# Two matmuls with a GELU between: eight of the opening's twelve loads move to GpSimd's queue and cast on the way

## The chip, the cores and the metric

The kernel runs on one core of a Trainium2 chip. The metric is the device time of one execution in microseconds (us), as the median of several runs. The profile is of one further execution on the same kind of chip.

## The reference

The inputs are `a` (1024 x 1024), `b` (1024 x 2048) and `c` (2048 x 1024), all float32. The kernel must compute

```python
h = np.matmul(a, b)
h = 0.5 * h * (1 + np.tanh(np.sqrt(2 / np.pi) * (h + 0.044715 * h ** 3)))
return np.matmul(h, c).astype(np.float32)
```

that is, a matmul, the tanh form of GELU, and a second matmul.

## The kernel before

**Stages.** All operands of matmuls are brought to bfloat16 (or to float32r for sums of blocks). The first matmul is made transposed: h's columns lie on the partitions, in 16 tiles of 128, in two halves of 512 rows of `a` each (`hT[0]`, `hT[1]`). The first four of the 16 tiles are made in the *opening*, by plain matmuls (`mm1`, `block`). The other twelve follow in two stages (`zero` for four tiles, `one` for eight), and the second matmul is a third stage (`two`). These three stages use a scheme of seven block products in place of eight (`Seven`, `seven`): sums and differences of blocks are made on VectorE and the products on TensorE (line 197).

**The opening.** `a` must be transposed, so that k lies on the partitions. It is loaded in eight pieces a(h, q): rows of half h, columns 256 q to 256 q + 255, which is two tiles of k. The left 512 columns of `b` are loaded in four pieces b(q) of two k tiles each. Before the change the twelve loads (512 KB each) all stand on SyncE's queue, in the order a(0,0), b(0), a(1,0), and then a(0,q), b(q), a(1,q) for q = 1, 2, 3 (lines 69 to 82). They land as float32 in `sta` and `stb`. From there

- `cast_a(h, q, engines)` casts a piece of `a` to bfloat16 into a small buffer `ab` (two of them), as a whole or in two halves on VectorE or ScalarE (lines 99 and 101);
- `turn(h, q, bank, ab)` transposes it on TensorE, four 128 x 128 blocks at a time, into a PSUM bank `pt` (line 132), and VectorE copies each of its two halves to `aT` (line 133). It is a generator: each `next` does one half, so that products can be put between the halves;
- `cast_b(k)` casts one k tile of `b` on ScalarE into `b1` (line 139);
- `block(h, tiles, ks)` issues the products of these k tiles for output tiles in banks `ps[h, t]` (line 105).

The order of all this is written out by hand (lines 214 to 294): for each q, products for half 0 with the k tiles 2q and 2q + 1, the two halves of turn(1, q), products for half 1, the two halves of turn(0, q + 1). Each engine runs its own instructions in the order in which they are written. `stir` issues products on a constant tile before the first data arrive. The banks: ps[0, 0..3] are banks 0 to 3, ps[1, 0..2] are banks 4 to 6; turn(0, 0) uses bank 4 before that, and nearly all others use bank 7 for both of their halves.

`zero.t1(4, part)` (line 155, on VectorE) makes the first difference of blocks from `aT`, a quarter at a time, between the turns of the opening.

**GpSimd's queue.** It holds a tiny copy into `gate` (line 84), which waits until a(1, 2) has landed, and behind it fourteen loads that cast from float32 to bfloat16 inside the transfer: two for the right half of `b1`, four for `b2` (lines 89 to 93), eight for `c_sb` (line 95). These need no cast on an engine.

Of the kernel before, what the change touches and what calls it, by code (L numbers as in the profile page):

```python
# [9 lines left out]
F32 = mybir.dt.float32  # L10
F32R = mybir.dt.float32r
BF16 = mybir.dt.bfloat16
# [7 lines left out]
def kernel(ctx, tc, a, b, c, out):  # L20
    nc = tc.nc
    M, K = a.shape
    _, N = b.shape
    _, P = c.shape
    H = 512
# [3 lines left out]
    av = a.rearrange("(mt p) k -> p mt k", p=128)  # L29
    bv = b.rearrange("(kt p) n -> p kt n", p=128)  # L30
# [9 lines left out]
    def slot(tag, shape, dt, name):  # L40
        return big.tile(shape, dt, name=name, tag=tag)

    def bank(i, shape=(128, H), dt=F32, name="ps"):
        return pp.tile(list(shape), dt, name=name, tag=f"bank{i}", padded_shape=None)

    def pieces(tag, bufs, shape, dt, name):
        return small.tile(shape, dt, name=name, tag=tag, bufs=bufs)
# [5 lines left out]
    gate = consts.tile([128, 1], F32, name="gate")  # L53
# [7 lines left out]
    b1 = slot("b1", [128, KT, 1024], BF16, "b1")  # L61
# [2 lines left out]

    KH = KT // 2
    stb = slot("x0", [128, KT, H], F32, "stb")
    sta = [slot(f"x{i}", [128, 2, 2, 4, 256], F32, "sta") for i in (1, 3)]

    def load_a(h, q):
        nc.sync.dma_start(out=sta[q // 2][:, h, q % 2],  # L70
                          in_=av[:, 4 * h:4 * h + 4, ds(q * 256, 256)])

    def load_b(q):
        nc.sync.dma_start(out=stb[:, 2 * q:2 * q + 2], in_=bv[:, 2 * q:2 * q + 2, 0:H])

    load_a(0, 0)
    load_b(0)
    load_a(1, 0)
    for q in range(1, 4):
        load_a(0, q)  # L80
        load_b(q)
        load_a(1, q)

    nc.gpsimd.tensor_copy(gate, sta[1][:, 1, 0, 3, 0:1])
    nc.scalar.activation(g, warm[:, 0:1], AF.Gelu_apprx_tanh)


    for k in range(0, KT, 4):
        nc.gpsimd.dma_start(out=b1[:, k:k + 4, H:], in_=bv[:, k:k + 4, ds(H, H)])
    for n in range(2):  # L90
        for k in range(0, KT, 4):
            nc.gpsimd.dma_start(out=b2[:, k:k + 4, ts(n, H)],
                                in_=bv[:, k:k + 4, ds(1024 + n * H, H)])
# [3 lines left out]
    def copy(eng, dst, src):  # L97
        if eng is nc.scalar:
            nc.scalar.activation(dst, src, AF.Copy)  # L99
        else:  # L100
            nc.vector.tensor_copy(dst, src)  # L101

    def mm1(p, t, h, ks):
        for k in ks:
            nc.tensor.matmul(p, b1[:, k, ts(t, 128)], aT[:, h, k],  # L105
                             start=(k == 0), stop=(k == KT - 1))
# [12 lines left out]
    def cast_a(h, q, *engs):  # L119

        ab = pieces("ab", 2, [128, 4, 256], BF16, "ab")
        for i, eng in enumerate(engs):
            w = 256 // len(engs)
            copy(eng, ab[:, :, ts(i, w)], sta[q // 2][:, h, q % 2][:, :, ts(i, w)])
        return ab

    def turn(h, q, i, ab):

        pt = bank(i, (128, 2, H), BF16, "pt")
        for n in range(2):  # L130
            for m in range(4):
                nc.tensor.transpose(pt[:, n, ts(m, 128)], ab[:, m, ts(n, 128)], ident)  # L132
            nc.vector.tensor_copy(aT[:, h, 2 * q + n], pt[:, n])  # L133
            yield

    def cast_b(k, n=1):
        for i in range(n):
            r = ds(i * (H // n), H // n)
            nc.scalar.activation(b1[:, k, r], stb[:, k, r], AF.Copy)  # L139

    def block(h, tiles, ks):
        for k in ks:
            for t in tiles:
                mm1(ps[h, t], t, h, (k,))
# [62 lines left out]
    def quarters(b, c0, w):  # L207
        return [[b[:, 0:4, ds(c0, w)], b[:, 4:8, ds(c0, w)]],
                [b[:, 0:4, ds(c0 + w, w)], b[:, 4:8, ds(c0 + w, w)]]]

    zero = Seven(4, quarters(b1, H, 256), BB, [None] * 4, [None] * 4, 2)
    one = Seven(4, quarters(b2, 0, H), BB, [None] * 4, zero.t)

    stir(256, 256, 256, 256)
    tn = turn(0, 0, 4, cast_a(0, 0, nc.vector))
    next(tn)
    stir(256)
    next(tn)
    stir(128)
    cast_b(0, 2)  # L220
    cast_b(1)
    ab = cast_a(1, 0, nc.vector, nc.scalar)
    block(0, range(4), (0,))
    block(0, range(2), (1,))
    tn = turn(1, 0, 7, ab)
    next(tn)
    block(0, range(2, 4), (1,))
    next(tn)
    for t in range(3):
        ps[1, t] = bank(4 + t)  # L230
    zero.t[0], zero.t[1] = pair(2)
    zero.t1(4, 0)
    ab = cast_a(0, 1, nc.scalar, nc.scalar)
    block(1, range(3), (0,))
    tn = turn(0, 1, 7, ab)
    next(tn)
    block(1, range(3), (1,))
    next(tn)
    cast_b(2)
    cast_b(3)  # L240
    ab = cast_a(1, 1, nc.vector, nc.scalar)
    block(0, range(4), (2,))
    block(0, range(1), (3,))
    tn = turn(1, 1, 7, ab)
    next(tn)
    block(0, range(1, 4), (3,))
    next(tn)
    zero.t1(4, 1)
    ab = cast_a(0, 2, nc.scalar, nc.scalar)
    block(1, range(3), (2,))  # L250
    tn = turn(0, 2, 7, ab)
    next(tn)
    block(1, range(3), (3,))
    next(tn)
    cast_b(4)
    cast_b(5)
    ab = cast_a(1, 2, nc.vector, nc.scalar)
    block(0, range(4), (4,))
    block(0, range(1), (5,))
    tn = turn(1, 2, 7, ab)  # L260
    next(tn)
    block(0, range(1, 4), (5,))
    next(tn)
    zero.t1(4, 2)
    ab = cast_a(0, 3, nc.scalar, nc.scalar)
    block(1, range(3), (4,))
    tn = turn(0, 3, 7, ab)
    next(tn)
    block(1, range(3), (5,))
    next(tn)  # L270
    zero.t1(4, 3)
    cast_b(6)
    cast_b(7)
    ab = cast_a(1, 3, nc.scalar, nc.vector)
    block(0, range(4), (6, 7))
    zero.t2(2, 0)
    for t in range(4):
        gelu(t, 0, ps[0, t])
    ps[1, 3] = bank(7)
    mm1(ps[1, 3], 3, 1, range(2))  # L280
    tn = turn(1, 3, 0, ab)
    next(tn)
    mm1(ps[1, 3], 3, 1, range(2, 5))
    next(tn)
# [210 lines left out]
```

## Time and profile before

| | us |
|---|---|
| Median of 8 runs | 118.21 (117.94 to 118.5) |
| The profiled execution | 118.3 |
| its span, first to last instruction | 116.5 |
| TensorE busy, share of the span | 111.1 (95%) |
| VectorE | 90.4 (78%) |
| ScalarE | 59.3 (51%) |
| GpSimd | 11.0 (9%) |

The granted clock of TensorE was at full speed in every slice of the span. DMA queues moved 17.91 MB; HBM was read for 20.97 MB, more than was written to the core's memory, since a casting load writes half of what it reads.

How to read the views: PE is TensorE (PEld its weight loads), DVE VectorE, ACT ScalarE, POOL GpSimd and SP SyncE; an engine's name with q is its instruction queue. A row of the timeline gives start and length in us, engine and line, operation, the tiles written and read, how often, and in brackets how long the engine stood idle before and what ended that. A row of the stage table gives for a stretch of time the busy time (and instructions) of TensorE, its weight loads, VectorE, ScalarE and GpSimd, then TensorE's clock, the busy share of the DMA engines and the GB/s that they wrote. The chain of work is followed back from the last instruction, at each step to what released it.

### The profile page before, as it was taken

What the parts mean: (1) busy time and instruction counts of PE and PEld (TensorE: products, weight loads), DVE (VectorE), ACT (ScalarE), POOL (GpSimd) and SP (SyncE); (2) the same over time, 40 slices, a digit from 0 to 9 for tenths busy, and PEclk for the clock granted to TensorE, in tenths of its full rate; (3) what the DMA queues carried; (4) which work ended last, traced back from release to release, by engine and by line L of the source; (5) the groups of instructions that cost most, each with busy time, mean ns of one, the idle gap of its engine ahead of it and who ended that gap; (6) DMA issues with size and microseconds to landing.
All of it is one profiled execution on the core that took longest, in us unless ns stands there. A gap on an engine that the chain in (4) does not pass through costs nothing.

```text
span 116.5 us, 1472 instructions
## 1 busy us (share of the span) xinstructions
PE 111.1 (95%) x534; PEld 76.6 (66%) x540; DVE 90.4 (78%) x107; ACT 59.3 (51%) x99; POOL 11.0 (9%) x21
## 2 busy tenths in 40 slices
PE   5989999999999999999999999999999999999980
PEld 4635455545777447888886444588888888888860
DVE  0336566899998999844789999999999986954670
ACT  5066678989369899066699329600033982000000
POOL 2000039723322000000000000000000000000000
PEclk9999999999999999999999999999999999999999
DMA  3999999999999999998000000070000002014993
GB/s 106 270 364 393 396 394 315 205 205 207 206 210 211 210 214 213 209 210 157 2 0 0 0 6 0 0 268 2 0 0 0 0 0 96 0 62 175 367 366 110
DMA packets 13542, 17.91 MB, mean 154 GB/s; under 512 B 736, under 2 KB 8928, under 8 KB 13536
## 3 DMA queue, kind: packets, MB, share of 16 engines
q0 software_dynamic: 5344, 7.34, 35.5%
q1 hardware_dynamic: 8192, 10.49, 25.1%
q8 instruction: 4, 0.07, 0.2%
q14 instruction: 2, 0.02, 0.0%
HBM read 20.97 MB, written 4.19 MB: 216 GB/s over the span
## 4 chain that ended last, share of the span: by engine, by line
PE 90%; DMA 5%; DVE 1%; issue 1%; SPq 0%; ACT 0%
PE ps L197 75%; PE ps L105 12%; DMA stb<-in_b_dram 5%; PE pt L132 3%; SPq L70 0%; DVE aT L133 0%; DVE ot L382 0%; ACT b L139 0%
## 5 line engine op out<-in xcount | busy, mean ns | idle before, releaser
L197 PE MATMUL ps<-x,s 128*128 128x512 f32 x128 | 29.6, 391 | 0.0
L197 PEld LDWEIGHTS ps<-x,s 128*128 128x128 f32 x128 | 24.0, 188 | 5.1
L197 PE MATMUL ps<-x,x 128*128 128x512 f32 x96 | 22.9, 394 | 0.0
L197 PEld LDWEIGHTS ps<-x,x 128*128 128x128 f32 x96 | 18.0, 188 | 3.9
L105 PE MATMUL ps<-aT,b 128*128 128x512 bf16 x62 | 15.8, 379 | 0.7 <-ACT b L139 0.5
L305 ACT ACTIVATE v<-ps 128x512 f32<-128x512 f32 x10 | 6.0, 598 | 19.4 <-PE ps L197 19.4
L197 PE MATMUL ps<-c_sb,hT 128*128 128x512 bf16 (+1 forms) x70 | 14.1, 355 | 0.1
L197 PE MATMUL ps<-x 128*128 128x512 f32 x56 | 13.2, 392 | 0.0
L197 PEld LDWEIGHTS ps<-x 128*128 128x128 f32 x56 | 10.2, 188 | 2.7 <-ACT u L305 0.4
L197 PEld LDWEIGHTS <-hT 128*128 128x128 bf16 x72 | 6.9, 98 | 7.0 <-issue 0.5
L133 DVE COPY aT<-pt 128x512 bf16<-128x512 bf16 x16 | 6.8, 423 | 6.0 <-PE pt L132 6.0
L109 ACT ACTIVATE hT<-ot 128x512 bf16<-128x512 f32 x18 | 10.5, 625 | 1.5 <-DVE ot L310 1.3
L310 DVE TENSOR_TENSOR ot<-ps,u 128x512 f32<-128x512 f32 x10 | 6.8, 690 | 5.2 <-ACT u L305 5.1
L310 DVE TENSOR_TENSOR ot<-ps,v 128x512 f32<-128x512 f32 x10 | 6.7, 688 | 5.2 <-DMA out_dram<-ot 3.8
L197 PE MATMUL ps<-aT,b 128*128 128x512 bf16 x46 | 10.6, 379 | 0.1
L155 DVE TENSOR_TENSOR x<-c_sb 128x1024 fp32r<-128x1024 bf16 x8 | 9.3, 1221 | 0.0
L105 PEld LDWEIGHTS <-b 128*128 128x128 bf16 x64 | 5.5, 98 | 4.8 <-ACT b L139 1.1
L197 PEld LDWEIGHTS <-b 128*128 128x128 bf16 x48 | 4.6, 98 | 5.7 <-issue 0.3
L132 PEld LDWEIGHTS <-ab 128*128 128x128 bf16 x64 | 4.6, 99 | 5.5 <-DVE ab L101 1.9
L99 ACT ACTIVATE ab<-sta 128x512 bf16<-128x512 f32 x10 | 6.0, 625 | 3.4 <-DMA sta<-in_a_dram 3.3
L305 ACT ACTIVATE u<-ps 128x512 f32<-128x512 f32 x10 | 5.9, 596 | 3.4 <-PE ps L197 3.2
L109 ACT ACTIVATE hT<-ps 128x512 bf16<-128x512 f32 x14 | 7.3, 596 | 0.4 <-PE ps L105 0.3
(39 smaller groups left out, 114.9 us busy)
## 6 DMA issues: line engine op xcount, KB each, us to landing
sta<-in_a_dram SPq DMA_DIRECT2D x8, 512.0 KB, 8.5
c_sb<-in_c_dram POOLq DMA_DIRECT2D x8, 512.0 KB, 19.8
b<-in_b_dram POOLq DMA_DIRECT2D x6, 512.0 KB, 11.3
out_dram<-ot SPq DMA_DIRECT2D x12, 256.0 KB, 2.1
stb<-in_b_dram SPq DMA_DIRECT2D x4, 512.0 KB, 8.2
out_dram<-ot SPq DMA_DIRECT2D x8, 128.0 KB, 2.0
```

The lines of the kernel that those rows point to most:

```text
L99: nc.scalar.activation(dst, src, AF.Copy)
L105: nc.tensor.matmul(p, b1[:, k, ts(t, 128)], aT[:, h, k], start=(k == 0), stop=(k == KT - 1))
L109: nc.scalar.activation(hT[h][:, t], p, AF.Gelu_apprx_tanh)
L132: nc.tensor.transpose(pt[:, n, ts(m, 128)], ab[:, m, ts(n, 128)], ident)
L133: nc.vector.tensor_copy(aT[:, h, 2 * q + n], pt[:, n])
L155: nc.vector.tensor_tensor(out=dst[:, r], in0=x[:, r], in1=y[:, r], op=op)
L197: nc.tensor.matmul(p[:, ds(c0, w)], l[:, k, ts(j, 128)], r[:, k, ds(c0, w)], start=(start and k == 0), stop=(k == self.kt - 1), skip_group ...
L305: nc.scalar.activation(st, p, AF.Copy)
L310: nc.vector.tensor_tensor(out=ot, in0=p, in1=st, op=ADD)
```

## The change

Only the first four loads, a(0,0), b(0), a(1,0) and a(0,1), stay on SyncE's queue and are cast on engines as before. The other eight go onto GpSimd's queue, ahead of the fourteen that were there, and cast inside the transfer: b pieces straight into `b1`, a pieces into a new bfloat16 tile `abq` (in the place of the second half of `sta`), from which `turn` reads directly. Their casts on ScalarE and VectorE are gone. The gate copy waits for b(0) in place of a(1, 2). `turn` can take two banks: turn(1, 0) puts its halves into banks 7 and 6 and both are issued one after the other, with the two products that stood between them behind both; the casts of a(0,1) and zero.t1 of the first quarter stand at slightly other places in the order. The rest of the opening keeps its order, written as a loop over q = 1, 2.

```diff
-    sta = [slot(f"x{i}", [128, 2, 2, 4, 256], F32, "sta") for i in (1, 3)]
...
-    load_a(0, 0)
-    load_b(0)
-    load_a(1, 0)
-    for q in range(1, 4):
-        load_a(0, q)
-        load_b(q)
-        load_a(1, q)
-
-    nc.gpsimd.tensor_copy(gate, sta[1][:, 1, 0, 3, 0:1])
+    sta = slot("x1", [128, 2, 2, 4, 256], F32, "sta")
+    abq = slot("x3", [128, 4, 2, 4, 256], BF16, "abq")
...
+    nc.sync.dma_start(out=sta[:, 0, 0], in_=a_part(0, 0))
+    nc.sync.dma_start(out=stb[:, 0:2], in_=b_part(0))
+    nc.sync.dma_start(out=sta[:, 1, 0], in_=a_part(1, 0))
+    nc.sync.dma_start(out=sta[:, 0, 1], in_=a_part(0, 1))
+
+    nc.gpsimd.tensor_copy(gate, stb[:, 1, 0:1])
     nc.scalar.activation(g, warm[:, 0:1], AF.Gelu_apprx_tanh)
 
 
+    def cast_load_a(h, q):
+        nc.gpsimd.dma_start(out=abq[:, q, h], in_=a_part(h, q))
+
+    def cast_load_b(q):
+        nc.gpsimd.dma_start(out=b1[:, 2 * q:2 * q + 2, 0:H], in_=b_part(q))
+
+    cast_load_b(1)
+    cast_load_a(1, 1)
+    for q in range(2, 4):
+        cast_load_a(0, q)
+        cast_load_b(q)
+        cast_load_a(1, q)
     for k in range(0, KT, 4):
         nc.gpsimd.dma_start(out=b1[:, k:k + 4, H:], in_=bv[:, k:k + 4, ds(H, H)])
...
     def turn(h, q, i, ab):
 
-        pt = bank(i, (128, 2, H), BF16, "pt")
+        banks = i if isinstance(i, tuple) else (i,)
+        pts = [bank(x, (128, 2, H), BF16, "pt") for x in banks]
         for n in range(2):
+            pt = pts[n % len(pts)]
...
     block(0, range(4), (0,))
     block(0, range(2), (1,))
-    tn = turn(1, 0, 7, ab)
-    next(tn)
+    for _ in turn(1, 0, (7, 6), ab):
+        pass
+    ab = cast_a(0, 1, nc.scalar, nc.scalar)
     block(0, range(2, 4), (1,))
-    next(tn)
     for t in range(3):
         ps[1, t] = bank(4 + t)
     zero.t[0], zero.t[1] = pair(2)
     zero.t1(4, 0)
-    ab = cast_a(0, 1, nc.scalar, nc.scalar)
     block(1, range(3), (0,))
     tn = turn(0, 1, 7, ab)
     next(tn)
     block(1, range(3), (1,))
     next(tn)
-    cast_b(2)
-    cast_b(3)
-    ab = cast_a(1, 1, nc.vector, nc.scalar)
...
+    for q in range(1, 3):
+        k = 2 * q
+        block(0, range(4), (k,))
+        block(0, range(1), (k + 1,))
+        tn = turn(1, q, 7, abq[:, q, 1])
+        next(tn)
+        block(0, range(1, 4), (k + 1,))
+        next(tn)
+        zero.t1(4, q)
+        block(1, range(3), (k,))
+        tn = turn(0, q + 1, 7, abq[:, q + 1, 0])
+        next(tn)
+        block(1, range(3), (k + 1,))
+        next(tn)
     zero.t1(4, 3)
-    cast_b(6)
-    cast_b(7)
-    ab = cast_a(1, 3, nc.scalar, nc.vector)
     block(0, range(4), (6, 7))
...
-    tn = turn(1, 3, 0, ab)
+    tn = turn(1, 3, 0, abq[:, 3, 1])
```

More of the change, by code (lines that the diff above doesn't have):

```diff
@@ L66, with a_part, b_part @@
     stb = slot("x0", [128, KT, H], F32, "stb")
-    sta = [slot(f"x{i}", [128, 2, 2, 4, 256], F32, "sta") for i in (1, 3)]
[L69 to L74, printed above, removed]
-    load_a(0, 0)
-    load_b(0)
-    load_a(1, 0)
-    for q in range(1, 4):
-        load_a(0, q)
-        load_b(q)
-        load_a(1, q)
-    nc.gpsimd.tensor_copy(gate, sta[1][:, 1, 0, 3, 0:1])
-    nc.scalar.activation(g, warm[:, 0:1], AF.Gelu_apprx_tanh)
+    sta = slot("x1", [128, 2, 2, 4, 256], F32, "sta")
+    abq = slot("x3", [128, 4, 2, 4, 256], BF16, "abq")
+    def a_part(h, q):
+        return av[:, 4 * h:4 * h + 4, ds(q * 256, 256)]
+    def b_part(q):
+        return bv[:, 2 * q:2 * q + 2, 0:H]
+    nc.sync.dma_start(out=sta[:, 0, 0], in_=a_part(0, 0))
[3 more added lines that the diff above has]
+    nc.gpsimd.tensor_copy(gate, stb[:, 1, 0:1])
+    nc.scalar.activation(g, warm[:, 0:1], AF.Gelu_apprx_tanh)
+    def cast_load_a(h, q):
[8 more added lines that the diff above has]
+        cast_load_a(1, q)
     for k in range(0, KT, 4):
@@ L123, in cast_a @@
             w = 256 // len(engs)
-            copy(eng, ab[:, :, ts(i, w)], sta[q // 2][:, h, q % 2][:, :, ts(i, w)])
+            copy(eng, ab[:, :, ts(i, w)], sta[:, h, q][:, :, ts(i, w)])
         return ab
     def turn(h, q, i, ab):
-        pt = bank(i, (128, 2, H), BF16, "pt")
+        banks = i if isinstance(i, tuple) else (i,)
+        pts = [bank(x, (128, 2, H), BF16, "pt") for x in banks]
         for n in range(2):
+            pt = pts[n % len(pts)]
             for m in range(4):
@@ L238 @@
     next(tn)
-    cast_b(2)
-    cast_b(3)
-    ab = cast_a(1, 1, nc.vector, nc.scalar)
[L242 to L270, printed above, removed]
+    for q in range(1, 3):
[12 more added lines that the diff above has]
+        next(tn)
     zero.t1(4, 3)
-    cast_b(6)
-    cast_b(7)
-    ab = cast_a(1, 3, nc.scalar, nc.vector)
     block(0, range(4), (6, 7))
```

## The prediction

> **What bounds the kernel now.** I read the page first: how busy each engine is, and the chain of work that ended last.
>
> ```profile
> PE 111.1 (95%) x534; PEld 76.6 (66%) x540; DVE 90.4 (78%) x107; ACT 59.3 (51%) x99; POOL 11.0 (9%) x21
> ...
> PE 90%; DMA 5%; DVE 1%; issue 1%; SPq 0%; ACT 0%
> PE ps L197 75%; PE ps L105 12%; DMA stb<-in_b_dram 5%; PE pt L132 3%; SPq L70 0%; DVE aT L133 0%; DVE ot L382 0%; ACT b L139 0%
> ```
>
> TensorE carries 90% of the chain; the 5% of DMA is the wait for the first piece of b. So the change can win only where TensorE stands still in the opening. I next read the chain in order of time (start, length, what):
>
> ```profile
> 1.23 5.49 DMA stb<-in_b_dram
> ...
> 9.03 0.43 DVE aT L133
> 9.46 0.04 issue
> ...
> 11.44 0.29 PE pt L132 x4
> 11.72 0.12 issue
> 11.84 1.03 PE ps L105 x4
> ```
>
> After 7.2 us there are two holes: at 9.03 to 9.5 (the second half of turn(1,0) waits until VectorE has copied the first half out of the same bank) and before 11.84. From 11.84 to 25.1 TensorE runs without a gap worth naming; the stage table gives 17.62 us of TensorE work in the 17.90 us from 7.2 to 25.1. **So the ceiling of any gain after 7.2 us is about 0.3 us by that table, 0.5 us by the holes**, unless the first product itself starts earlier. The timeline of the opening shows what ends each wait:
>
> ```profile
> 9.70 1.15 ACT L99 ACTIVATE ab<-sta 128x512 bf16<-128x512 f32 x2 [0.96 <-DMA sta<-in_a_dram]
> ...
> 10.38 0.23 PEld L132 LDWEIGHTS <-ab 128*128 128x128 bf16 x4 [0.34 <-ACT ab L99]
> ...
> 10.93 1.15 ACT L139 ACTIVATE b<-stb 128x512 bf16<-128x512 f32 x2
> ...
> 13.71 1.15 ACT L99 ACTIVATE ab<-sta 128x512 bf16<-128x512 f32 x2 [0.72 <-DMA sta<-in_a_dram]
> ...
> 16.38 0.63 ACT L99 ACTIVATE ab<-sta 128x512 bf16<-128x512 f32 x1 [0.32 <-DMA sta<-in_a_dram]
> ...
> 16.45 1.62 POOL L89 DMA_DIRECT2D b<-in_b_dram  x2
> ...
> 17.73 1.15 ACT L99 ACTIVATE ab<-sta 128x512 bf16<-128x512 f32 x2 [0.72 <-DMA sta<-in_a_dram]
> ...
> 20.36 0.63 ACT L99 ACTIVATE ab<-sta 128x512 bf16<-128x512 f32 x1 [0.28 <-DMA sta<-in_a_dram]
> ...
> 23.58 0.70 POOL L95 DMA_DIRECT2D c_sb<-in_c_dram  x1 [1.14 <-DMA b<-in_b_dram]
> ...
> 26.12 0.71 POOL L95 DMA_DIRECT2D c_sb<-in_c_dram  x1 [1.83 <-DMA b<-in_b_dram]
> ```
>
> An instruction that waited for a DMA marks the landing. Load 4, a(0,1), lands at 9.65. A load of a takes 1.35 us of the stream (16.38 to 17.73), a load of b 1.28 (20.36 less 17.73 is 2.63 for one of each). GpSimd's casting loads of 1 MB land 2.54 us apart (23.58, 26.12).
>
> **Two banks for turn(1,0).** Removed: the wait at 9.26 to 9.51 of the timeline, 0.25 us. But TensorE then meets the transposes of a(0,1), which already waited 0.34 us for ScalarE's cast; that cast started at 9.70 because load 4 had just landed. Load 4 stays fourth on the same queue, so these transposes stay at 10.38. Alone, this edit is worth about 0. Its second bank, 6, is also ps[1,2]: the copy out of it ends about 9.9 and the first product into it is due at 9.95, so it costs nothing. VectorE's zero.t1 (0.68 us, ran to 10.95 and held up the next copy) runs 0.4 us earlier, so that copy starts 0.05 us sooner.
>
> **Casts removed.** By the means of their rows ScalarE loses six casts of b (0.614 us each, 3.7) and seven half casts of a (0.625, 4.4), VectorE three (0.43, 1.3). Nearly all of it lies beside TensorE, which hardly waits after 11.84, and is worth nothing. On the path lies one: b tile 2 was cast at 10.93 to 11.5, and the products behind the transposes of 11.34 started 0.50 us after those (11.84), where the same pair elsewhere needs 0.22 (12.84 to 13.07, 13.75 to 13.97). Without the cast: 11.34 - 0.05 + 0.22 = 11.5. **Gain 0.3 us**, if b(1) has landed.
>
> **Loads moved.** SyncE's queue keeps four; GpSimd gets eight issues ahead of its fourteen, 0.70 to 0.81 us each (its rows), some 6 us, faster than their transfers. All of them queue behind the gate copy, which now waits for the first b piece: that lands at 6.72, and from the landing of the copy's old load (copy at 16.33) to the issue at 16.45 went 0.2 us, so 6.9. The upper half of b and c queue behind these eight. The ninth GpSimd load had to wait for the landing of the first (the row at 23.58); now the ninth is issued near 13, after b(1), and waits for nothing.
> When does b(1) land? The unknown is the start-up of GpSimd's first transfer. Before, it was issued at 16.45, and written bytes per second (a casting load writes half of what it reads) show when it moves:
>
> ```profile
> 18.75:19.00 0.25, 0.25 (x5) 0.25 (x5) 0.25 (x1) 0.20 (x2) 0.25 (x2) 1.00 1.13 377
> ...
> 19.25:19.50 0.25, 0.25 (x2) 0.10 (x1) 0.25 (x1) 0.25 (x2) 0.25 (x1) 1.00 1.32 311
> ...
> 20.25:20.50 0.25, 0.25 (x3) 0.10 (x1) 0.25 (x2) 0.14 (x1) 0.25 (x2) 1.00 1.25 201
> ```
>
> Up to 19.0 all is SyncE's (377 GB/s), and GpSimd's takes over as that queue drains. Start-up is thus at most 2.8 us: ready by 9.7, as load 4 ends. From SyncE's last landing (20.3) to GpSimd's first (23.5) went 3.2 us for a 2.54 us transfer, so the handover costs 0.1 to 0.65. b(1) is half of one: 9.65 + 1.27 + 0.3 = 11.2 (11.0 to 11.6), due at 11.5.
> The a loads now write 512-byte rows, which the trace lacks. The nearest rows: 2 KB rows of c and 1 KB rows of b move at the same 205 to 214 GB/s written (page, slices); on SyncE's queue halving the row costs 5% (1.35 against 1.28). So 1.27 x 1.05 = 1.33 us. Lower end 1.27; upper end, a row of 512 bytes priced as one of 1 KB, 2.54.
> Landings then: a(1,1) 12.5, a(0,2) 13.9, b(2) 15.1, a(1,2) 16.5, a(0,3) 17.8, b(3) 19.1, a(1,3) 20.4. Due, 0.3 ahead of the old starts of their first readers in TensorE's rows (all of TensorE's later work queues behind such a reader): 12.5, 14.35, 15.5, 16.6, 18.4, 19.55, 21.7. All in time, two barely, because the cast that stood between landing and use is gone. The upper half of b follows at 22.9 and 25.5; before, 23.5 and 26.1.
>
> **Against a rule.** The Trainium skill, "DMA: Bandwidth & Descriptors", section "Queues, rings and completion order", says each DMA engine serves its queues in turn, packet by packet. With the 1 us to the first byte that the page gives such loads, GpSimd's first would be ready at 6.9 + 0.8 + 1.0 = 8.7, share the engines with the last 0.9 us of load 4, and make it 0.9 us late (an estimate from that page). The row above speaks for the other: 2.5 us after the issue SyncE's queue still had the full rate, and its landings 16.38, 17.73, 20.36 did not spread. It cannot exclude a start-up that just ended then. I take the row.
>
> **Sum.** 0.3 us off the 118.3 us of the profiled execution (span 116.5 and 1.8 around): 118.0; off the median of 118.21: **117.9**. The gain passes to the end: behind 25.1 TensorE is busy 87.95 of 88.20 us, and VectorE, whose queue is dense there, is itself 0.3 to 0.4 us earlier by its removed casts.
>
> **Rivals.**
> 1. *The wait is moved, not removed*: landings 0.3 late eat the gain; 118.2, no change. For: margins of 0 to 0.1 at two loads. Part of the forecast's spread.
> 2. *Small rows cost more* (slower). Place: the five a loads on GpSimd's queue. By a(1,2), the third, an extra x us each delays TensorE by 3x - 0.1. From 1.46 us a load the gain is gone; at 1.66 us (a packet of 512 bytes at 52 ns instead of 41) the delay is 0.9: 118.2 - 0.3 + 0.9 = 118.8. At the upper end of 2.54 us a(1,3) comes 4.7 us late, 122.6. Against: the rows above show hardly a price per packet.
> 3. *Queues in turn* (the rule): a(0,1) 0.9 late, less the 0.3: 118.8. Against: the flat 377 GB/s.
> 4. *The start moves too.* From 4.0 to 6.0 us the stream ran at 184 to 309 GB/s instead of 385, some 0.28 MB or 0.7 us lost before b(0). If issuing eight more loads caused it, b(0) and load 4 come 0.7 us earlier: 117.2. Against: the four that stay are the first in the same order, and later loads were issued just as slowly at full rate.
>
> **Chances.** A change within 0.2% (0.24 us) can't be told from none. Forecast 0.52 (own range 117.7 to 118.2; 0.40 of it faster, 0.12 same), rival 1 to its full size 0.06 (same), rival 2 0.22, rival 3 0.10, rival 4 0.10. Faster 0.50, same 0.18, slower 0.32. The range takes in half of rival 4 and nearly all of 2 and 3 below the upper end: 117.3 to 119.2.
>
> **What would show it.** Right: transposes of a(0,1) still near 10.4; the first product on b tile 2 near 11.5 with no wait for DMA; TensorE without holes to 24.8. Wrong: weight loads of b or abq waiting for GpSimd's DMAs, growing from load to load (rival 2), or starting with ScalarE's cast at 10.5 (rival 3); or a first product well before 7.2 (rival 4).

## The result, and the profile after

The changed kernel takes 119.05 us (median of 20 runs, 118.39 to 119.62), the kernel before 118.28 us in the runs beside it: a ratio of 1.0063 (95% interval 1.0051 to 1.0075). It is slower by 0.75 us where 0.3 us of gain was forecast. (The ratios here and below leave out executions more than 1.5% above the fastest of the same kernel, among them two of the four of run 8 and one of the four of run 9.) The profiled execution after took 119.62 us (span 117.9), the slowest of its 20, so its losses are those of a bad case; that of before took 118.3 (span 116.5).

The page's shares of the chain of work:

```profile
PE 85%; DMA 10%; POOL 1%; issue 0%; DVE 0%; SPq 0%
PE ps L208 74%; PE ps L114 8%; DMA abq<-in_a_dram 5%; DMA stb<-in_b_dram 5%; PE pt L143 2%; POOL b L89 1%; DVE ot L371 0%; SPq L76 0%; POOL gate L81 0%
```

A second DMA, `abq`, is now on the chain with 5%, as large as the wait for b(0). The chain in order of time says which:

```profile
6.94 0.18 POOL gate L81
7.12 0.76 POOL b L89
7.88 6.30 DMA abq<-in_a_dram
...
14.23 0.40 PE pt L143 x4
```

It runs from b(0) through the gate copy and GpSimd's first issue to the load of a(1,1), issued at 7.88 and landed at 14.18. Only then do its transposes start, 1.39 us later than the 12.84 of before, where they waited for a cast on VectorE:

```profile
12.84 0.23 PEld L132 LDWEIGHTS <-ab 128*128 128x128 bf16 x4 [0.46 <-DVE ab L101]
```

The timeline after:

```profile
7.06 0.83 POOL L89 DMA_DIRECT2D b<-in_b_dram  x1
...
10.43 0.30 PEld L143 LDWEIGHTS <-ab 128*128 128x128 bf16 x4 [0.25 <-ACT ab L108]
...
13.13 1.03 PE L114 MATMUL ps<-aT,b 128*128 128x512 bf16 x4 [1.33 <-DMA b<-in_b_dram]
...
14.22 0.23 PEld L143 LDWEIGHTS <-abq 128*128 128x128 bf16 x4 [0.56 <-DMA abq<-in_a_dram]
...
14.46 0.74 POOL L98 DMA_DIRECT2D b<-in_b_dram  x1 [0.57 <-DMA abq<-in_a_dram]
...
15.80 0.74 POOL L101 DMA_DIRECT2D b<-in_b_dram  x1 [0.59 <-DMA abq<-in_a_dram]
17.07 0.74 POOL L101 DMA_DIRECT2D b<-in_b_dram  x1 [0.53 <-DMA b<-in_b_dram]
```

The transposes of a(0,1) stand at 10.43, as forecast. The first product on b tile 2 waits for b(1) until 13.13 (forecast 11.5), the transposes of a(1,1) for theirs. GpSimd's last rows mark landings: its tenth load waits for the second, and so on. They follow 1.34 us (14.46 to 15.80, a piece of a) and 1.27 us (to 17.07, a piece of b) apart, the forecast pace. So only the first two transfers are late; the rest follow in step, TensorE consumes at the same pace, and the delay never closes. The stages behind cost the same: the chain has 88.04 us from the first stage product to the last row before (25.26 to 113.30) and 88.01 after (26.62 to 114.63).

The stage table of the changed kernel shows the two late transfers:

```profile
9.50:11.50 2.00, 2.00 (x16) 0.99 (x14) 1.67 (x4) 1.15 (x2) 2.00 (x3) 1.00 0.98 99
12.50:14.50 2.00, 1.30 (x9) 0.68 (x11) 0.00 (x0) 0.00 (x0) 1.33 (x3) 1.00 1.43 197
```

From 9.5 to 11.5 GpSimd's stream runs at half the rate that it has from 12.5 on. Fewer packets are in flight (a DMA share of 0.98 against 1.43), and each takes longer: by the single packets in the trace, those of b(1), of 1 KB written, took 145 ns on average, against 98 ns for later ones of the same size. Two microseconds at half rate are 1 us of stream lost.

### The profile page after: what moved, and what is told of

Same layout as the page of the kernel before. It is cut to its first block, busy times and chain, and to the rows that moved or that the text cites. A ratio compares the mean times of both kernels' runs of the same rounds, so it can differ in the third digit from the quotient of the medians.

```text
span 117.9 us, 1447 instructions
## 1 busy us (share of the span) xinstructions
PE 111.6 (95%) x534; PEld 77.2 (66%) x540; DVE 89.4 (76%) x104; ACT 51.8 (44%) x86; POOL 16.9 (14%) x29
## 4 chain that ended last, share of the span: by engine, by line
PE 85%; DMA 10%; POOL 1%; issue 0%; DVE 0%; SPq 0%
PE ps L208 74%; PE ps L114 8%; DMA abq<-in_a_dram 5%; DMA stb<-in_b_dram 5%; PE pt L143 2%; POOL b L89 1%; DVE ot L371 0%; SPq L76 0%; POOL gate L81 0%
## 5 line engine op out<-in xcount | busy, mean ns | idle before, releaser
L118 ACT ACTIVATE hT<-ot 128x512 bf16<-128x512 f32 x18 | 10.5, 625 | 1.4 <-DVE ot L299 1.3
L104 POOL DMA_DIRECT2D c_sb<-in_c_dram x8 | 5.7, 712 | 12.4 <-DMA b<-in_b_dram 11.7
L166 DVE TENSOR_TENSOR x<-b 128x1024 fp32r<-128x1024 bf16 (+1 forms) x4 | 7.0, 1752 | 0.1
```

What stands on the lines that cost most here:

```text
L104: nc.gpsimd.dma_start(out=c_sb[:, t:t + 2], in_=cv[:, t:t + 2])
L118: nc.scalar.activation(hT[h][:, t], p, AF.Gelu_apprx_tanh)
L166: nc.vector.tensor_tensor(out=dst[:, r], in0=x[:, r], in1=y[:, r], op=op)
```

## The experiments

Theory **slow start**: GpSimd's first two transfers need some 6.9 us from the first issue, whatever is done, and the change issues them too late for that to lie behind SyncE's queue. Rivals: the **two banks** have a part in it; **queues in turn** (a GpSimd transfer slows SyncE's); the **first use** of the queue; making further **descriptors** (the orders for the DMA engines, taken here to be made in GpSimd's issue rows of 0.7 to 0.8 us each) while the first transfers run; **b's rows**. The small rows of a were ruled out by the landings above. Times are medians beside the kernel before on the same chip, 118.19 to 118.32 us. No kernel changes what is computed.

**1. The banks alone** (the kernel before with the change's turn(1,0) and its order):

```diff
-    tn = turn(1, 0, 7, ab)
-    next(tn)
+    for _ in turn(1, 0, (7, 6), ab):
+        pass
+    ab = cast_a(0, 1, nc.scalar, nc.scalar)
     block(0, range(2, 4), (1,))
-    next(tn)
```

> The kernel before with the order and the two banks of turn(1,0) of the change, all loads as before. All theories: the wait of 0.25 us ahead of the second half of turn(1,0) goes, but the transposes of a(0,1) stay at 10.4 us behind load 4, so 118.2 to 118.3, no change; in the profile the first product on b tile 2 near 11.8.

118.28 us, ratio 1.0003 (0.9995 to 1.0011). No change; the transposes of a(0,1) again waited for ScalarE's cast:

```profile
11.18 0.23 PEld L134 LDWEIGHTS <-ab 128*128 128x128 bf16 x4 [0.41 <-ACT ab L99]
```

The profiled execution (119.01 us) is the slowest of its 15, and b(0) was 0.66 us later in it than before. Counted from the first product, the transposes start after 3.30 us, against 3.16 before.

**2. The loads alone** (that edit undone in the changed kernel):

```diff
-    for _ in turn(1, 0, (7, 6), ab):
-        pass
-    ab = cast_a(0, 1, nc.scalar, nc.scalar)
+    tn = turn(1, 0, 7, ab)
+    next(tn)
     block(0, range(2, 4), (1,))
+    next(tn)
...
+    ab = cast_a(0, 1, nc.scalar, nc.scalar)
     block(1, range(3), (0,))
```

> The change with one bank for turn(1,0) and the order of before; only the loads are moved. If the loads carry the whole loss: 119.0, as the changed kernel, with b(1) landing near 12.7 us. If the two banks had a part in it: nearer to 118.3.

119.03 us, 1.0061 (1.0046 to 1.0076): the whole loss. Its profile (118.92 us) is nearer to the usual run than that of the change. There b(1) came in time (the five products that begin with b tile 2 did not wait for a load), and the wait is for a(1,1):

```profile
11.63 1.24 PE L114 MATMUL ps<-aT,b 128*128 128x512 bf16 x5
...
13.56 0.23 PEld L143 LDWEIGHTS <-abq 128*128 128x128 bf16 x4 [1.18 <-DMA abq<-in_a_dram]
```

13.56 less 12.84 is 0.72 us, about the measured loss (0.77).

**3. The gate on the first load**, so that GpSimd issues 2 us earlier:

```diff
-    nc.gpsimd.tensor_copy(gate, stb[:, 1, 0:1])
+    nc.gpsimd.tensor_copy(gate, sta[:, 0, 0, 3, 0:1])
```

> The change with the gate copy reading a(0,0) instead of b(0): GpSimd issues from 4.3 us on, not 7.1. Theory 'slow start' (GpSimd's first transfer needs about 2 us to its first byte and has slow packets for 2 us more, hidden if its descriptors are ready before SyncE's queue drains): b(1) lands near 11.2, TensorE does not wait, 117.9 to 118.1. Rival 'queues in turn' (a ready GpSimd transfer takes engine time from SyncE's): a(1,0) and a(0,1) land up to 1 us later, 118.8 to 119.3.

117.73 us, 0.9961 (0.9947 to 0.9975): faster than both kernels. Timeline and stage table:

```profile
4.99 0.83 POOL L89 DMA_DIRECT2D b<-in_b_dram  x1
...
11.93 0.37 PEld L143 LDWEIGHTS <-abq 128*128 128x128 bf16 x4 [0.17 <-DMA abq<-in_a_dram]
...
12.09 0.39 PE L143 MATMUL pt<-ident,abq 128*128 128x128 bf16 x4
```

```profile
9.50:11.50 2.00, 2.00 (x17) 1.06 (x16) 1.33 (x4) 0.84 (x2) 2.00 (x4) 1.00 1.38 188
```

The half rate is gone (188 GB/s against 99), a(1,1) is there at 11.9, 6.9 us after GpSimd's first issue, and its transposes start at 12.09, 0.75 us ahead of the kernel before. This profiled run was a good one (117.46 us), with b(0) 0.4 us early; what is left, 0.3 us, has the size forecast for the removed cast. Load 4 was not delayed. GpSimd was busy issuing in all of these 2 us (2.00), so the making of descriptors is not enough to halve the rate.

**4. Six loads on SyncE's queue** (b(1) and a(1,1) too, cast on engines as before):

```diff
+    nc.sync.dma_start(out=stb[:, 2:4], in_=b_part(1))
+    nc.sync.dma_start(out=sta[:, 1, 1], in_=a_part(1, 1))
...
-    cast_load_b(1)
-    cast_load_a(1, 1)
...
+    cast_b(2)
+    cast_b(3)
+    ab = cast_a(1, 1, nc.vector, nc.scalar)
```

> The change with six loads on SyncE's queue: b(1) and a(1,1) too, cast on engines as in the kernel before; GpSimd's six others are issued from 7.1 us on. Slow start: hidden behind SyncE's queue, which drains near 12.3; a(0,2) lands near 13.9, TensorE does not wait for DMA, 118.1 to 118.3 (the 0.3 us wait for the cast of b tile 2 is back). Queues in turn: b(1) and a(1,1) late by up to 1.3 us, 118.9 to 119.4.

119.11 us, 1.0078 (1.0066 to 1.0090), against slow start's number and for the rival's. The cause is in one row:

```profile
13.02 0.63 ACT L108 ACTIVATE ab<-sta 128x512 bf16<-128x512 f32 x1 [1.08 <-DMA sta<-in_a_dram]
```

a(1,1), now SyncE's last load, landed at 13.0 instead of 12.3, and the cast still stands behind it. GpSimd's transfers, issued from 6.76 on, sent their first packet at 10.80, before SyncE's were through, and the rate written fell:

```profile
9.50:11.00 1.50, 1.50 (x11) 0.68 (x10) 1.22 (x4) 1.36 (x3) 1.50 (x3) 1.00 1.08 381
11.50:12.50 1.00, 1.00 (x7) 0.38 (x5) 0.42 (x1) 0.44 (x1) 1.00 (x2) 1.00 1.41 209
```

**5. No gate at all** (GpSimd issues at 1.48):

```diff
-    nc.gpsimd.tensor_copy(gate, stb[:, 1, 0:1])
+    nc.gpsimd.tensor_copy(gate, warm[:, 0:1])
```

> The change with a gate copy that waits for no load: GpSimd issues from about 1.5 us on. Theory 'SyncE first' (an engine serves GpSimd's queue only when SyncE's part on it is done, as with the gate on a(0,0), where the first GpSimd packet came at 8.2 us as SyncE's queue drained): b(0) still lands at 6.2 to 7.2 and load 4 near 9.3, 117.6 to 118.0. Rival 'queues in turn': b(0) lands 1.5 to 2.5 us later, and the time is 119.5 to 120.5.

121.59 us, 1.0277 (1.0249 to 1.0305). Timeline and stage table:

```profile
10.21 0.63 ACT L108 ACTIVATE ab<-sta 128x512 bf16<-128x512 f32 x1 [1.90 <-DMA sta<-in_a_dram]
...
13.38 1.15 ACT L108 ACTIVATE ab<-sta 128x512 bf16<-128x512 f32 x2 [2.54 <-DMA sta<-in_a_dram]
```

```profile
6.00:6.50 0.50, 0.50 (x3) 0.21 (x2) 0.15 (x1) 0.00 (x0) 0.50 (x2) 1.00 1.03 301
...
8.00:8.50 0.50, 0.50 (x4) 0.22 (x3) 0.00 (x0) 0.31 (x1) 0.00 (x0) 1.00 1.19 249
```

From 6 to 9 us the rate written falls to 249 GB/s, between the 385 of SyncE's loads alone and the 197 of casting loads alone. By the single packets in the trace the two queues are served about equally: from 7.5 to 10.5 us SyncE's started 451 packets and GpSimd's 446. a(1,0) lands at 10.1 instead of 8.1, a(0,1) at 13.3 instead of 9.6. **Queues in turn is right** once GpSimd's transfers flow, and "SyncE first" is false. b(0) was not late (its first product at 7.54), since GpSimd's first packet came only at 5.84, 4.4 us after its issue. The time lies 1.1 us beyond the rival's range, and b(0), which it expected late, was on time.

**6. A pause after b(1)**, so that no descriptors are made meanwhile:

```diff
     cast_load_b(1)
+    nc.gpsimd.tensor_copy(g2, sta[:, 0, 1, 3, 0:1])
     cast_load_a(1, 1)
```

> The change with a second small copy on GpSimd, between the issues of b(1) and a(1,1), that waits for a(0,1) (about 9.5 us): no descriptors are made while b(1) starts. If making the later descriptors slows the packets of b(1): b(1) lands near 11.6 instead of 12.7, and TensorE starts on it a microsecond earlier. If the slow start has nothing to do with it: b(1) as late as in the changed kernel, a(1,1) later still, 119.2 to 120.0.

122.2 us, 1.0334 (1.0284 to 1.0383). This is beyond both expectations. b(1) was in time (product at 11.52, no wait), but so it was in run 2 without a pause. Its packets took 112 ns on average, against 137 in run 2; with one profile of each, that does not decide it. In its timeline

```profile
9.77 1.50 POOL L87 DMA_DIRECT2D abq<-in_a_dram  x2
...
13.78 0.23 PEld L145 LDWEIGHTS <-abq 128*128 128x128 bf16 x4 [1.52 <-DMA abq<-in_a_dram]
```

a(1,1), issued 2 us later than in run 2, is used only 0.2 us later. Another slow stretch followed, which cost the rest:

```profile
12.50:14.50 2.00, 0.97 (x9) 0.48 (x8) 0.28 (x1) 0.00 (x0) 2.00 (x4) 1.00 1.34 179
14.50:16.00 1.50, 1.23 (x9) 0.47 (x7) 1.02 (x3) 0.00 (x0) 1.50 (x3) 1.00 0.98 65
```

So a slow stretch need not lie at the start. GpSimd's queue was empty before a(1,1) (0 to 4 GB/s at 10.75 to 11.25), yet the rate was 176 GB/s by 12.0 and fell only at 14.25.

**7. A tiny casting load first**, at the very start, into an unused tile:

```diff
+    first = consts.tile([128, 16], BF16, name="first")
+    nc.gpsimd.dma_start(out=first, in_=a.rearrange("(mt p) k -> p mt k", p=128)[:, 0, 0:16])
```

> The change with one more tiny casting load (128 rows of 64 bytes, not used) issued on GpSimd's queue at the very start; the gate as in the change, so the other loads are issued at the same time. If the first use of the queue is what is slow: b(1) lands near 11.3, 118.0. If it is that the queue starts empty at the moment when SyncE's drains: as the changed kernel, 119.0.

119.04 us, 1.0059 (1.0026 to 1.0092), as the changed kernel. The tiny load was issued at 1.42 us, and the half rate is still there, so the first use is not the cause:

```profile
9.50:11.50 2.00, 2.00 (x15) 0.87 (x14) 1.47 (x4) 1.15 (x2) 2.00 (x4) 1.00 0.96 98
```

**8. a(1,1) ahead of b(1)** on GpSimd's queue, and **12. b(1) as two loads** of 256 columns, so that all rows are alike:

```diff
-    cast_load_b(1)
     cast_load_a(1, 1)
+    cast_load_b(1)
```

```diff
-    cast_load_b(1)
+    for i in range(2):
+        nc.gpsimd.dma_start(out=b1[:, 2:4, ts(i, 256)], in_=bv[:, 2:4, ts(i, 256)])
```

> The change with a(1,1) ahead of b(1) on GpSimd's queue. If the slow packets belong to the start of the queue: a(1,1) takes them, it lands near 12.7 and b(1) near 14, so TensorE waits some 1.3 us more than in the changed kernel and the time is 120.2. If they belong to b's rows: a(1,1) lands near 11.2 and b(1) near 13.5.

> The change with b(1) as two loads of 256 columns each (rows of 1 KB read, 512 bytes written, like those of a), the rest as in the change. Question: why are b(1)'s packets slow when GpSimd's queue starts? If long rows are slow at a start: the halves run at 60 ns a packet, b(1) lands near 11.3, 118.0 to 118.3. If it is b's layout (rows 8 KB apart in memory, whatever their length) or the start itself: still slow, b(1) at 12 to 13, one issue of 0.75 us more ahead of a(1,1), 119.0 to 119.8.

Run 8 took 119.36 and 119.56 us in the two executions compared, ratio 1.0097 (1.0057 to 1.0137); run 12 took 119.69 us, 1.0102 (1.0073 to 1.0130). The profile of run 8 is of its longest execution (121.98 us), in which TensorE's clock fell to 0.52 from 14 us on, behind the stretches shown. The stage tables, 8 first:

```profile
9.00:10.00 1.00, 1.00 (x9) 0.41 (x6) 1.00 (x3) 0.61 (x2) 1.00 (x3) 1.00 1.35 180
10.50:11.50 1.00, 0.91 (x8) 0.40 (x5) 0.48 (x2) 0.04 (x1) 1.00 (x2) 1.00 1.08 132
```

```profile
9.00:10.00 1.00, 1.00 (x10) 0.52 (x8) 0.89 (x3) 0.45 (x1) 1.00 (x3) 1.00 1.10 141
10.50:11.50 1.00, 1.00 (x10) 0.58 (x9) 0.42 (x1) 0.20 (x1) 1.00 (x3) 1.00 0.86 79
```

In both, the first GpSimd transfer ran well, and the slow stretch came over the second: b(1) in run 8, where TensorE waited for it until 13.84, a(1,1) in run 12, which was used at 14.05. The landings of run 8 alone fit the expectation for b's rows, though not its time. In run 12 the halves of b(1) began at 60 ns a packet, as expected for short rows, and b(1) was in time, but the time is that of the other expectation. So the slow stretch belongs neither to the first transfer alone nor to long rows alone. That b's rows have no part in it is not shown: in run 8 the 1 KB packets, b(1)'s, took 140 ns on average (98 is usual), the 512-byte packets of a's pieces 65 (60 is usual).

**9. b(0) third on SyncE's queue**, gate as in run 3. The stream of every run is slow once more, at 4 to 6 us (252 GB/s in the changed kernel); this asks whether by time or by piece:

```diff
-    nc.sync.dma_start(out=stb[:, 0:2], in_=b_part(0))
     nc.sync.dma_start(out=sta[:, 1, 0], in_=a_part(1, 0))
+    nc.sync.dma_start(out=stb[:, 0:2], in_=b_part(0))
```

> The gate on a(0,0) as in the faster run, and on SyncE's queue a(1,0) ahead of b(0). Question: does the slow stretch of the first 2.5 us of loads (200 to 280 GB/s from 4 to 6 us in every run so far) belong to the first piece of b, or to the time? If to b's first piece: it moves to 5.3 to 7.5 us and b(0) lands 1.3 us later than before, near 8.0; the first product starts near 8.2. If to the time: a(1,0) is slow and b(0) lands at the same 8.0 but the rate is low at 4 to 6 us. Time 118.3 to 119.0 in both, since the first product waits for b(0) but a(1,0) is there earlier.

120.63 us, 1.0166 (1.0119 to 1.0214), worse than expected.

```profile
4.00:5.00 1.00, 0.97 (x3) 0.25 (x1) 0.67 (x1) 0.00 (x0) 0.64 (x1) 1.00 1.07 380
5.50:6.50 1.00, 0.97 (x8) 0.62 (x7) 0.51 (x2) 0.00 (x0) 1.00 (x2) 1.00 0.75 225
9.00:10.00 1.00, 0.90 (x3) 0.35 (x4) 0.00 (x0) 1.00 (x4) 1.00 (x2) 0.50 1.21 228
```

On SyncE's queue the slow stretch does belong to b(0): 380 GB/s at 4 to 5 us, 225 at 5.5 to 6.5. TensorE waited 2.46 us for b(0), until 9.1 us, and had half of its clock (0.50) from about 8.4 to about 12. The one execution with the clock at 1.000 throughout took 119.13 us, close to the expected 119.0, so the extra loss goes with the clock. (In the profile of run 8 the clock halved as well, after a wait of 2.44 us; after one of 2.02 us in run 10 it stayed at 1.00.)

**10. The gate later**, on a(1,0):

```diff
-    nc.gpsimd.tensor_copy(gate, stb[:, 1, 0:1])
+    nc.gpsimd.tensor_copy(gate, sta[:, 1, 0, 3, 0:1])
```

> The change with the gate on a(1,0), 1.3 us later than b(0): GpSimd issues from 8.4 us on, its first packet near 10.2. If the loss is the lateness of the issue plus a slow first b piece: b(1) near 13.2 to 13.7, a(1,1) near 14.8, the time 1.0 to 1.4 us above the changed kernel, 120.0 to 120.4. If the slow packets belong to a time (9 to 12 us) and not to the start: b(1) near 12.7, at most 119.5.

121.16 us, 1.0264 (1.0246 to 1.0281), 0.8 us beyond the first number but on its side. Timeline and stage table:

```profile
8.32 0.83 POOL L89 DMA_DIRECT2D b<-in_b_dram  x1
...
15.44 0.23 PEld L143 LDWEIGHTS <-abq 128*128 128x128 bf16 x4 [1.50 <-DMA abq<-in_a_dram]
```

```profile
9.00:10.00 1.00, 1.00 (x9) 0.40 (x5) 1.00 (x3) 0.64 (x2) 1.00 (x3) 1.00 0.12 8
```

Here SyncE's queue is empty from 9 us, and the bare start-up shows: issued at 8.32, next to nothing moved until 10 (8 GB/s; the first packet came at 9.86, 1.5 us after the issue began). a(1,1) is used at 15.44.

**11. Run 3 with one bank** for turn(1,0) and the order of before (the edits of 2 and 3 together).

> The gate on a(0,0), and turn(1,0) in one bank with the order of before. With the two banks this gave 117.73. If load 4 and its cast set the start of the transposes of a(0,1) here too: the same, 117.7 to 117.8. If the two banks matter once the loads come in time: 117.9 to 118.0 (0.25 us of wait is back).

118.01 us beside 118.19, the second number, but scattered (117.81 to 119.24): ratio 1.0000 (0.9980 to 1.0019), no change shown. This interval and that of run 3 (0.9947 to 0.9975) do not meet, so with one bank the earlier issue removes the loss but is not shown to gain on the kernel before. In its profile the transposes of a(1,1) wait 0.43 us for their load until 12.59, so not the bank but the landing sets the time there too. Whether two banks are part of run 3's gain is left open.

**Together.** From GpSimd's first issue to the first transposes of a(1,1), and from those to the end of the span, in the profiles:

| | first issue | transposes of a(1,1) | between | span | span less transposes |
|---|---|---|---|---|---|
| before | 16.45 (other loads) | 12.84 | | 116.5 | 103.7 |
| after | 7.06 | 14.22 | 7.2 | 117.9 | 103.7 |
| 2, loads alone | 6.77 | 13.56 | 6.8 | 117.1 | 103.5 |
| 3, gate first | 4.99 | 12.09 | 7.1 | 115.7 | 103.6 |
| 10, gate later | 8.32 | 15.44 | 7.1 | 119.1 | 103.7 |
| 11, gate first, one bank | 5.09 | 12.59 | 7.5 | 116.2 | 103.6 |
| 6, pause | 6.79 | 13.78 | 7.0 | 119.8 | 106.0 |
| 7, tiny load first | 6.79 | 13.96 | 7.2 | 117.6 | 103.6 |
| 12, b(1) in halves | 6.82 | 14.05 | 7.2 | 118.0 | 103.9 |

But for run 6, with its second slow stretch, the last column is nearly constant: all of the difference is in when a(1,1) can be transposed. The column "between" nearly is too: moving the issue moves the landing with it. That holds from 5 to 8.3 us; with the issue at 1.48 (run 5) the time is set by SyncE's late loads.

## Why the prediction was wrong

- **The ceiling and the casts** (0.3 us to gain from the cast of b tile 2): right in kind. Run 3, where the loads come in time, gains 0.53 us; part of it is b(0) earlier in that profile, which one profile can't divide.
- **Two banks worth 0 with the loads of before**: right (run 1).
- **"When does b(1) land?"**: the step that failed. From a start-up of at most 2.8 us and a handover of 0.1 to 0.65 us it took 11.2 for b(1), and so 12.5 for a(1,1), 2.9 us after SyncE's last landing. Measured from that landing (9.75) to a(1,1)'s, it was 4.4 us; in runs 2 and 7, which lose about the same time, it was 4.1 and 4.2. There b(1) was in time, so the term that came out too small is the time of the first two transfers together: the prediction took them at full pace from the first byte on. The handover came from the row of before in which GpSimd's first transfer took over from SyncE's queue without a gap. But that transfer had been issued at 16.45, 2.4 us before its first packet, and had ample time to get ready. The change issues at 7.06, with SyncE's last load landing at 9.7. The start-up itself was within the bound (the first packet came 1.5 us after the issue, in run 10 as in the change); what the trace of before could not show, and the prediction put at nothing, is the half rate of the next 2 to 3 us. The profile held a warning: from GpSimd's first issue to its first landing before went 7.1 us (16.45 to 23.58), of which the prediction put the first 2.8 down to SyncE's queue.
- **Pace of small rows** (1.33 us): right, 1.34 measured; rival 2 is out.
- **"I take the row" against queues in turn**: wrong as a reading, though without weight for this time. The flat 377 GB/s did not show that SyncE's queue goes first, only that GpSimd's transfer had not started. Its first packet came later beside a full queue (2.4 us after the issue before, 4.0 in run 4) than the 1.8 us of the prediction's estimate; with SyncE's queue running out it came after 1.5 us. Runs 4 and 5 (in run 5, 451 packets of one queue beside 446 of the other) bear out the Trainium skill, "DMA: Bandwidth & Descriptors", "Queues, rings and completion order": the engines then serve both. In the change load 4 was not late (the transposes of 10.43), so rival 3 is not what happened.
- **Rival 1** named the right place, late landings, but capped them at 0.3 us; the case that came, the same place with 0.7 to 1.4 us, had no chance of its own. **Rival 4**: no; b(0) landed at 6.89 in the chain, not earlier.
- **The range**: 119.05 us lies within the stated 117.3 to 119.2, but that range reached so far for rivals 2 and 3, and neither happened. That it fits is luck.

**What stays open** is why the packets are slow. What the traces add is when. Where GpSimd's first packet came 2.4 to 4.4 us after the first issue, with SyncE's queue still full in between (before, runs 3, 4, 5, 9, 11), the 1 KB packets of its first b piece took 96 to 112 ns on average. Where it came 1.4 to 1.6 us after the issue (after, runs 2, 7, 8, 10), they took 135 to 146. Run 6, with its pause, lies between (1.7 us, 112 ns). So a lead goes with faster packets, but no run tells how.

- It is not the first use (7), and neither the first transfer alone nor long rows alone (8, 12).
- Making descriptors alone does not do it (3: GpSimd issuing without a break at 188 GB/s), though the pause of run 6 leaves open that it has a part. An empty queue alone does not do it either (6).
- VectorE seems to get in GpSimd's way (last section), and may slow the making of descriptors. No run was made for this. The rates do not follow VectorE at the same moment: in run 8, 180 GB/s with VectorE busy for 1.00 us of 1.00, and 132 with 0.48.
- Whether a DMA engine that meets a half-filled queue, or memory that is read by the engines in step, is behind it, no run tells.

## What to carry to other kernels

A casting load from GpSimd's queue is as fast as another once it flows (1.27 to 1.34 us for 512 KB read, against 1.28 to 1.35 on SyncE's queue), but here its first two transfers took about 7 us from the first issue. In this kernel an issue at 5 us, 7 us ahead of the first reader of the second load and with SyncE's loads still running for 3 us, was early enough; one at 7 us was too late. Issued at 1.5 us it came too early: once both queues flow they share the engines, and the loads that everybody waits for come late (121.6 us). For another kernel, measure the lead instead of taking these numbers over. A handover seen in a trace is only a bound for one with the same lead time.

## What the runs showed that was not expected

- GpSimd seems to wait for VectorE. In runs 3, 9 and 11 the gate copy of one element a partition took 0.70 us and ended with the cast on VectorE beside it, against 0.18 in the changed kernel, where it ran beside no cast. The other way round it is less clear: VectorE's cast of a half piece took 0.59 us beside GpSimd's issues in the changed kernel and 0.43 before, but 0.43 beside such issues in runs 7 and 11 too. The row of run 3 (the cast on VectorE ran from 4.31 to 5.00):

```profile
4.34 0.70 POOL L81 COPY gate<-sta 128x1 f32<-128x1 f32 x1 [3.04 <-DMA sta<-in_a_dram]
```

- The first piece of b is slow on SyncE's queue too, in every run; by the prediction's estimate it costs some 0.7 us ahead of the first product, and in the one profile of run 9 it moves with the piece. Why is open.
